# A hybrid decoder layer on one core: the order of wide and narrow products inside a projection block

## The chip, the core and the metric

The kernel runs on one core of a Trainium2 chip. A core has a matmul engine (TensorE, PE in the profile, with its weight loads shown as PEld), three elementwise engines (VectorE = DVE, ScalarE = ACT, GpSimd = POOL), queues of DMA transfers, an on-chip memory for operands, and a small accumulator memory (PSUM) that only matmuls accumulate in. The metric is the device time of one execution in microseconds. The median of three runs of the kernel before is 733.31 us (732.69 to 734.17).

A matmul here has a stationary operand of 128 x 128, loaded by an instruction of its own (LDWEIGHTS), and a moving operand of up to 512 columns. "Wide" below is a product with 512 moving columns, "narrow" one with 256.

## The reference

One decoder layer on 256 tokens of width 1024, in float32: a SwiGLU feed-forward, then a mixer with two branches side by side (Mamba-2 in chunks, and differential attention), merged by gates, then a second SwiGLU feed-forward; normalizations stand around each.

```python
def swiglu(x, w_gate, w_up, w_down):
    return (jax.nn.silu(x @ w_gate) * (x @ w_up)) @ w_down
...
    h = h + 0.5 * rmsnorm(swiglu(rmsnorm(h, ffn1_pre_g[l]), ...), ffn1_post_g[l])
    u = rmsnorm(h, mix_pre_g[l])
    z, xbc, dt_raw, q, k, v, gate_logits = jnp.split(u @ w_in[l], IN_SPLITS, axis=-1)
...
    h = h + rmsnorm(merged @ w_out[l], mix_post_g[l])
    h = h + 0.5 * rmsnorm(swiglu(rmsnorm(h, ffn2_pre_g[l]), ...), ffn2_post_g[l])
```

`xbc` holds the Mamba branch's x, B and C. The hidden width of the feed-forwards is 2816.

## The kernel before

**Precision.** Every float32 operand of a large product is split in two parts in a shorter matmul format (fp32r): hi is the rounded value, lo the rest. A product is then hi x hi + hi x lo + lo x hi. Weights are split on the core as they arrive: a chunk of 1 MB lands in a `raw` buffer (L240, on SP's queue), ScalarE casts each half to `whi` (L258), VectorE subtracts to give `wlo` (L259). Both halves lie in a ring of 29 equal buffers (`k4`), and `take` (L305) keeps the splitting three chunks ahead of use.

**The blocks in question.** The function `mm_w` (L334) makes the transposed output of one weight chunk of 1024 rows and 256 columns, in two blocks of 128 columns (`m`). The contraction runs over eight tiles `j`; `whi` and `wlo` each come as two halves of four tiles. The activations lie as hi and lo side by side, so that one wide product with `whi` as the stationary operand makes hi x hi in the left half of the accumulator and hi x lo in the right half (L342). A narrow product with `wlo` as the stationary operand adds lo x hi to the left half (L344). A block is eight wide products, then eight narrow ones, and an eviction: ScalarE copies the right half (L346 or L349), VectorE adds the left half (L347 or L350). Accumulators come from a PSUM ring of three (`pj`).

**Who calls it.** `mm_w` is called for gate and up of both feed-forwards (9 chunks each of gate and up, tiles `pg_f` and `pup_f`), for B and C (4 chunks, `pbc`), for x (8 chunks, `pxs`) and for q and k (4 chunks each, `pq` and `pk`): 56 chunks, 112 blocks. The other large products run elsewhere: V, the merge gates, the branch and output projections through `mm_nat` (L361), z through `mm_t` (L329 to L332, narrow products only), the first columns of gate and up of the first feed-forward through `mm_both` (L377), and the down projections through `mm_quads` (L718) and `mm_n` (L640). All of these but z use wide products.

**Order.** In parts of the program the order on TensorE is that of the source (`own_order`); in the parts where `mm_w` is called a scheduler orders the instructions of each engine, by dependencies and by times that it assumes. Between the projections of the mixer, pieces of other work (the chunked scan, the norms) are handed in by `back.run` (L1454) with a share of time each, and their matmuls stand between or inside blocks. Within a queue each engine issues in order.

Of the kernel before, what the change touches and what calls it, by code (L numbers as in the profile page):

```python
# [30 lines left out]
KD = D // P  # L31
# [23 lines left out]
def tile_hybrid_layer(ctx: ExitStack, tc: tile.TileContext, x, ffn1_pre_g, ffn1_w_gate, ffn1_w_up,  # L55
# [25 lines left out]
    def pj(name):  # L81

        return ps.tile([P, 512], F32, tag="pj", name=name, bufs=3)
# [250 lines left out]
    def mm_w(dst, name, w, act, scale=None):  # L334


        (wh, wl), (ah, _, ahl) = w, act
        for m in range(2):
            acc = pj(f"{name}{m}")
            cs = slice(m * P, (m + 1) * P)  # L340
            for j in range(KD):
                nc.tensor.matmul(acc, wh(j)[:, cs], ahl(j), start=j == 0, stop=False)  # L342
            for j in range(KD):
                nc.tensor.matmul(acc[:, :T], wl(j)[:, cs], ah(j), start=False, stop=j == KD - 1)  # L344
            if scale is None:
                nc.scalar.copy(dst[:, m, :], acc[:, T:])  # L346
                nc.vector.tensor_tensor(dst[:, m, :], acc[:, :T], dst[:, m, :], ALU.add)  # L347
            else:
                nc.scalar.activation(dst[:, m, :], acc[:, T:], AF.Copy, scale=scale)  # L349
                nc.vector.scalar_tensor_tensor(dst[:, m, :], acc[:, :T], scale, dst[:, m, :], ALU.mult, ALU.add)  # L350
# [483 lines left out]
    def ffn(post_v, tag, ready, turned, then, products):  # L834
# [28 lines left out]
        for j in range(2, FF // T):  # L863
            if j % 2 == 0:
                gh = k4([P, 4, T], f"gh_{tag}{j}", F32R)
                gl = k4([P, 4, T], f"gl_{tag}{j}", F32R)
            o = (j % 2) * 2
            gu += [(gh[:, o + m, :], gl[:, o + m, :]) for m in range(2)]
            sg = k2([P, 2, T], f"sg_{tag}{j}")
            mm_w(sg, f"pg_{tag}{j}", take(), act_u)  # L870
            act(sg, sg, AF.Silu)
            su = k2([P, 2, T], f"su_{tag}{j}")
            mm_w(su, f"pup_{tag}{j}", take(), act_u)
            nc.vector.tensor_tensor(sg, su, sg, ALU.mult)  # L874
            split(gh[:, o:o + 2, :], gl[:, o:o + 2, :], sg)
            if j // 2 in QUADS[tag]:
                if j % 2:
                    sums[j // 2] = sums_of(j // 2, even, sg)
                else:
                    even = sg  # L880
# [306 lines left out]
    for i in range(4):  # L1187
        acc = k2([P, 2, T], f"bc{i}")
        mm_w(acc, f"pbc{i}", take(), act_u)
        dst = (bT, cT)[i // 2]  # L1190
        conv(acc, 16 + 2 * i, dst[:, (i % 2) * 2:(i % 2) * 2 + 2, :])
        if i == 1:
            cumulated()
# [442 lines left out]
```

## Time and profile before

| | |
|---|---|
| median of three runs | 733.31 us |
| the profiled execution | 732.92 us |
| its span, first to last instruction | 731.1 us |
| mean granted TensorE clock | 0.997 |
| TensorE busy | 723.8 us, 4025 matmuls |
| VectorE busy | 607.6 us |
| ScalarE busy | 473.4 us |
| DMA | 137.92 MB, mean 189 GB/s |

Rows that group instructions give line, engine, operation, output and inputs by the program's names, shape, count, then busy time in us, the mean duration of one in ns, and the idle time before them. Rows in order of time give the start in us from the span's start, the length, and the same names; neighbours of one kind are merged with their count. Matmuls are pipelined: a product's duration is longer than the distance from its start to the next start, which is called its spacing below, and a busy TensorE is not one at its peak.

### The profile page before, as it was taken

The numbers are of one execution on the slowest core, as the hardware profiler recorded it, in microseconds if no ns is written. First come the engines' busy times: TensorE is split into PE (matmuls) and PEld (weight loads), VectorE is DVE, ScalarE is ACT, GpSimd is POOL, SyncE is SP. The second block draws the span as 40 slices with busy tenths as digits, with TensorE's granted clock in tenths as the row PEclk, the third lists the DMA queues.
The fourth block names the chain that finished last, engine by engine and source line by source line (L and its number), as shares of the span: only waits on it lengthen the run. The fifth ranks groups of instructions, "written<-read, shape, count | busy, mean of one in ns | idle before, by whom it ended". The sixth has DMA issues, their size and how long they took to land.

```text
span 731.1 us, 10546 instructions
## 1 busy us (share of the span) xinstructions
PE 723.8 (99%) x4025; PEld 620.9 (85%) x4025; DVE 607.6 (83%) x931; ACT 473.4 (65%) x805; POOL 31.3 (4%) x63
## 2 busy tenths in 40 slices
PE   9999999999999999999999999999999999999996
PEld 8888888888878889999888788888888888888885
DVE  6978788999979989777996997784784878779995
ACT  5657566656867676869965577782663757566562
POOL 4300000000200000000000000000010000000000
PEclk9999999999999999999999999999999999999998
DMA  8874645466673557675564664364461754654551
GB/s 296 235 261 147 225 158 188 173 225 264 184 227 119 172 173 226 206 226 180 158 221 148 203 220 144 144 243 190 126 240 37 231 193 155 228 203 146 181 189 57
DMA packets 94451, 137.92 MB, mean 189 GB/s; under 512 B 2669, under 2 KB 68801, under 8 KB 94401
## 3 DMA queue, kind: packets, MB, share of 16 engines
q1 hardware_dynamic: 91728, 129.51, 53.3%
q0 software_dynamic: 2368, 7.22, 3.3%
q8 instruction: 31, 0.51, 0.3%
q10 hardware_dynamic: 304, 0.53, 0.2%
q14 instruction: 20, 0.16, 0.1%
HBM read 136.17 MB, written 1.08 MB: 188 GB/s over the span
## 4 chain that ended last, share of the span: by engine, by line
PE 99%; DVE 0%; ACT 0%; DVEq 0%; issue 0%; ACTq 0%
PE pg_f L342 9%; PE pup_f L342 9%; PE pws L361 6%; PE pgt L361 6%; PE acc_f2p L718 5%; PE acc_f1p L718 5%; PE pup_f L344 5%; PE pg_f L344 5%; PE pxs L342 4%; PE pn_f L377 3%; PE acc_mx L640 3%; PE pn_mx L361 3%; PE pn_f L361 3%; PE pwd L361 3%; PE acc_f1p L640 2%; PE acc_f2p L640 2%
## 5 line engine op out<-in xcount | busy, mean ns | idle before, releaser
L259 DVE TENSOR_TENSOR wlo<-raw,whi 128x1024 fp32r<-128x1024 f32 x216 | 258.0, 1221 | 20.0 <-ACT whi L258 18.9
L258 ACT CAST whi<-raw 128x1024 fp32r<-128x1024 f32 x216 | 219.2, 1049 | 13.6 <-DMA raw<-in_ffn_w_down_dram 2.8
L342 PE MATMUL pg_f<-u_f,whi 128*128 128x512 f32 x288 | 72.9, 393 | 0.0
L342 PE MATMUL pup_f<-u_f,whi 128*128 128x512 f32 x288 | 72.1, 392 | 0.0
L342 PEld LDWEIGHTS pup_f<-u_f,whi 128*128 128x128 f32 x288 | 51.9, 189 | 9.5 <-issue 0.2
L342 PEld LDWEIGHTS pg_f<-u_f,whi 128*128 128x128 f32 x288 | 51.8, 189 | 9.2
L344 PEld LDWEIGHTS pg_f<-u_f,wlo 128*128 128x128 f32 x288 | 39.3, 190 | 2.8
L344 PEld LDWEIGHTS pup_f<-u_f,wlo 128*128 128x128 f32 x288 | 39.3, 190 | 2.8
L344 PE MATMUL pup_f<-u_f,wlo 128*128 128x256 f32 x288 | 40.2, 282 | 0.0
L344 PE MATMUL pg_f<-u_f,wlo 128*128 128x256 f32 x288 | 40.1, 282 | 0.0
L130 ACT CAST wqh<-wt 128x1024 fp32r<-128x1024 f32 x24 | 25.3, 1054 | 22.9 <-DVE wt L122 22.8
L346 ACT COPY su_f<-pup_f 128x256 f32<-128x256 f32 x36 | 13.4, 371 | 36.9 <-PE pup_f L344 36.9
L347 DVE TENSOR_TENSOR su_f<-pup_f,su_f 128x256 f32<-128x256 f32 x36 | 15.2, 421 | 24.9 <-ACT su_f L346 24.9
L361 PE MATMUL pgt<-whi,u_mx 128*128 128x512 f32 x128 | 33.1, 393 | 0.0
L342 PE MATMUL pxs<-u_mx,whi 128*128 128x512 f32 x128 | 32.4, 395 | 0.0
L329 PE MATMUL pz<-u_mx,whi 128*128 128x256 f32 x128 | 31.6, 284 | 0.0
L330 PE MATMUL pz<-u_mx,whi 128*128 128x256 f32 x128 | 31.5, 283 | 0.0
L135 DVE TENSOR_TENSOR wql<-wt,wqh 128x1024 fp32r<-128x1024 f32 x24 | 29.3, 1221 | 0.2
L361 PEld LDWEIGHTS pgt<-whi,u_mx 128*128 128x128 f32 x128 | 23.6, 188 | 5.3 <-issue 0.7
L342 PEld LDWEIGHTS pxs<-u_mx,whi 128*128 128x128 f32 x128 | 23.0, 189 | 4.1
L319 ACT CAST gh_f<-sg_f 128x512 fp32r<-128x512 f32 x18 | 11.2, 621 | 23.3 <-DVE sg_f L874 23.3
L135 DVE TENSOR_TENSOR wql<-raw,wqh 128x1024 fp32r<-128x1024 f32 x18 | 21.8, 1221 | 4.4 <-ACT wqh L130 4.4
(413 smaller groups left out, 1593.3 us busy)
## 6 DMA issues: line engine op xcount, KB each, us to landing
raw<-in_w_in_dram SPq DMA_DIRECT2D x40, 1024.0 KB, 5.2
raw<-in_ffn_w_down_dram SPq DMA_DIRECT2D x22, 1024.0 KB, 4.8
raw<-in_ffn_w_gate_dram SPq DMA_DIRECT2D x20, 1024.0 KB, 5.4
raw<-in_ffn_w_up_dram SPq DMA_DIRECT2D x20, 1024.0 KB, 5.1
raw<-in_ssd_w_branch_dram SPq DMA_DIRECT2D x8, 1024.0 KB, 4.9
acb<-acd POOLq DMA_DIRECT2D x8, 512.0 KB, 5.1
raw<-in_da_w_branch_dram SPq DMA_DIRECT2D x4, 1024.0 KB, 5.1
raw<-in_w_out_dram SPq DMA_DIRECT2D x4, 1024.0 KB, 4.8
```

Source lines behind the costliest of these rows:

```text
L130: nc.scalar.copy(hi, src)
L135: nc.vector.tensor_sub(lo, src, hi.bitcast(F32))
L258: last_cast[0] = behind(nc.scalar.copy(hi, r[:, js, :]), "cast").ins
L259: m = nc.vector.tensor_sub(lo, r[:, js, :], hi.bitcast(F32))
L329: nc.tensor.matmul(acc[m], wh(j)[:, cs], ah(k0 + j), start=first and j == ks[0], stop=False)
L330: nc.tensor.matmul(acc[m], wh(j)[:, cs], al(k0 + j), start=False, stop=False)
L342: nc.tensor.matmul(acc, wh(j)[:, cs], ahl(j), start=j == 0, stop=False)
L344: nc.tensor.matmul(acc[:, :T], wl(j)[:, cs], ah(j), start=False, stop=j == KD - 1)
L361: nc.tensor.matmul(acc, a(k0 + j), b(j), start=first and i == 0, stop=last and i == 11)
L377: nc.tensor.matmul(accs[b], x_(k0 + j), w_(j), start=first and j == 0 and w_ is wh and x_ is acts[b][0], stop=last and j == 3 and w_ is wl)
L640: nc.tensor.matmul(acc[b][q][:, cs] if to is None else to, x_[:, ts], w_(kt)[:, halves[q]][:, cs], start=to is not None and kt == 0 and x_ ...
L718: nc.tensor.matmul(bank[p], x_, w_, start=p not in begun, stop=last and p in (1, 5, 6, 7))
```

## The change

One line is removed, and with it one loop:

```diff
             for j in range(KD):
                 nc.tensor.matmul(acc, wh(j)[:, cs], ahl(j), start=j == 0, stop=False)
-            for j in range(KD):
                 nc.tensor.matmul(acc[:, :T], wl(j)[:, cs], ah(j), start=False, stop=j == KD - 1)
```

The wide product with `whi` and the narrow one with `wlo` of the same `j` now follow each other directly. A block reads wide, narrow, wide, narrow, eight times, and the last narrow product of a block is followed by the first wide one of the next. The number of products, their operands and their shapes stay the same; only the order of the additions into the left half changes. In the changed file all lines behind L342 have a number one lower, so the narrow products are at L343.

## The prediction

> **What bounds the kernel now.** I read the page first, then the waits of TensorE, then the groups by line, and last the order of time inside single blocks.
>
> ```profile
> span 731.1 us, 10546 instructions
> PE 723.8 (99%) x4025; PEld 620.9 (85%) x4025; DVE 607.6 (83%) x931; ACT 473.4 (65%) x805; POOL 31.3 (4%) x63
> PE 99%; DVE 0%; ACT 0%; DVEq 0%; issue 0%; ACTq 0%
> PE warm L451 <- DVE zeros L434: 1.1, 1, 1.1
> ```
>
> The first two rows are the span and the busy times. The third is the chain that ended last: TensorE is 99% of it. The fourth is the whole answer to "for whom did TensorE wait": one wait of 1.1 us at the very start. So the time is the sum of the spacings of the matmuls, and a change of their order can act only in two ways: through the spacing of neighbours, or by making TensorE wait for something that it now finds ready.
>
> The products that the change moves are these six groups at L342, each with as many at L344:
>
> ```profile
> L342 PE MATMUL pg_f<-u_f,whi 128*128 128x512 f32 x288 | 72.9, 393 | 0.0
> L342 PE MATMUL pup_f<-u_f,whi 128*128 128x512 f32 x288 | 72.1, 392 | 0.0
> L342 PE MATMUL pxs<-u_mx,whi 128*128 128x512 f32 x128 | 32.4, 395 | 0.0
> L342 PE MATMUL pbc<-u_mx,whi 128*128 128x512 f32 x64 | 16.4, 397 | 0.0
> L342 PE MATMUL pk<-u_mx,whi 128*128 128x512 f32 x64 | 16.4, 395 | 0.0
> L342 PE MATMUL pq<-u_mx,whi 128*128 128x512 f32 x64 | 16.3, 394 | 0.0
> L344 PE MATMUL pup_f<-u_f,wlo 128*128 128x256 f32 x288 | 40.2, 282 | 0.0
> ```
>
> 288 + 288 + 128 + 3 x 64 = 896 pairs of a wide (512) and a narrow (256) product, in 112 blocks of 8 pairs. One nanosecond on a pair is 0.9 us.
>
> **What a pair costs today.** From the order of time, a block's start and the start of the block 32 blocks later (in the first feed-forward, nothing between them but such blocks):
>
> ```profile
> 37.08 2.00 PE L342 MATMUL pup_f<-u_f,whi 128*128 128x512 f32 x8
> 38.92 1.11 PE L344 MATMUL pup_f<-u_f,wlo 128*128 128x256 f32 x8
> 39.87 0.40 PE L342 MATMUL pup_f<-u_f,whi 128*128 128x512 f32 x1
> ...
> 126.47 2.00 PE L342 MATMUL pup_f<-u_f,whi 128*128 128x512 f32 x8
> ```
>
> (126.47 - 37.08) / 32 = 2.793 us for a block, 349.2 ns for a pair: 1.84 us / 8 = 230 for a wide one, 0.95 us / 8 = 119 for a narrow one.
>
> **What each width costs when nothing changes around it.** A stretch of wide products only (24 starts from 24.78 to 30.22), and a stretch of narrow ones only (24 starts from 286.05 to 288.93):
>
> ```profile
> 24.78 1.98 PE L377 MATMUL pn_f<-whi,raw_u 128*128 128x512 f32 x8
> 30.22 0.62 PE L342 MATMUL pg_f<-u_f,whi 128*128 128x512 f32 x2
> L377 PE MATMUL pn_f<-whi,raw_u 128*128 128x512 f32 x15 | 3.9, 389 | 0.0
> ...
> 286.05 0.28 PE L329 MATMUL pz<-u_mx,whi 128*128 128x256 f32 x1
> 288.93 0.28 PE L329 MATMUL pz<-u_mx,whi 128*128 128x256 f32 x1
> L332 PE MATMUL pz<-u_mx,wlo 128*128 128x256 f32 x8 | 1.1, 283 | 0.0
> ```
>
> 5.44 us / 24 = 226.7 ns a wide one, shown with a duration of 389; 2.88 / 24 = 120.0 a narrow one, shown with 283. Duration less spacing is 162 or 163 in both, so a single product's spacing can be read off its duration. Together the steady prices make 346.7, 2.5 less than today's pair. The block at 62.22 shows where the 2.5 are (its first five wide products, one window each):
>
> ```profile
> L342 PE MATMUL pup_f<-u_f,whi 128*128 128x512 f32 x1 | 0.4, 396 | 0.0
> L342 PE MATMUL pup_f<-u_f,whi 128*128 128x512 f32 x1 | 0.4, 398 | 0.0
> L342 PE MATMUL pup_f<-u_f,whi 128*128 128x512 f32 x1 | 0.4, 389 | 0.0
> L342 PE MATMUL pup_f<-u_f,whi 128*128 128x512 f32 x1 | 0.4, 395 | 0.0
> L342 PE MATMUL pup_f<-u_f,whi 128*128 128x512 f32 x1 | 0.4, 393 | 0.0
> ```
>
> After a run of narrow products the wide ones cost 234, 236, 227, 233, 231 and then the settled 227. A disturbance outlives its cause by several products. The first narrow one after a settled wide one is cheap:
>
> ```profile
> L344 PE MATMUL pup_f<-u_f,wlo 128*128 128x256 f32 x1 | 0.3, 278 | 0.0
> ```
>
> 278 - 163 = 115, and the rest of its run is back at 120. So there is a settled price (wide 227, narrow 114) and a disturbed one (wide 231 to 236, narrow 120), some 6.5 ns apart for either width; a wide product needs about five of its kind to settle, one narrow product unsettles.
>
> **The change, step by step.** It removes and adds no instruction. Inside a block the order wide x8, narrow x8 becomes wide, narrow, eight times.
>
> *Spacing.* A wide product now always follows a narrow one, so it never gets the five it needs. I price it as disturbed for good. The row for that is the sum-products of the first feed-forward's down projection, where wide products alone are disturbed for 24 in a row:
>
> ```profile
> 134.82 0.63 PE L718 MATMUL acc_f1p<-wqh,s 128*128 128x512 f32 x2
> ...
> 140.42 0.39 PE L718 MATMUL acc_f1p<-wqh,gh_f 128*128 128x512 f32 x1
> ```
>
> (140.42 - 134.82) / 24 = 233.3 each. The narrow one follows a wide product that isn't settled. Two places show such a first narrow product: behind a single wide one at 368.4, and behind three at 32.5, in this order:
>
> ```profile
> L344 PE MATMUL pk<-u_mx,wlo 128*128 128x256 f32 x1 | 0.3, 281 | 0.0
> L344 PE MATMUL pg_f<-u_f,wlo 128*128 128x256 f32 x1 | 0.3, 285 | 0.0
> ```
>
> 281 - 163 = 118 and 285 - 163 = 122: not the cheap 115 that follows a settled one. I take their mean, 120, which is also the steady narrow price. The pair is then 233.3 + 120 = 353.3, against 349.2: +4.1 ns, times 896 = **+3.7 us**. No row of before alternates the widths, so the bounds: from below both settled, 226.7 + 114 = 340.7, -8.5 x 896 = -7.6 us; from above the dearest of each shown here, 236 + 122 = 358, +8.8 x 896 = +7.9 us. I take 353.3 because in every row here a product that follows a narrow or an unsettled one is disturbed.
>
> *Waits.* The first narrow product of a chunk now comes one wide product after the chunk's start (0.23 us), not eight (1.84), so half 0 of wlo is needed 1.6 us sooner; half 1 is needed after four pairs, 1.4 us, not 2.3. The split runs well ahead. The chunk whose block starts at 59.42 gets its wlo here:
>
> ```profile
> 48.73 1.22 DVE L259 TENSOR_TENSOR wlo<-raw,whi 128x1024 fp32r<-128x1024 f32 x1
> 50.20 1.22 DVE L259 TENSOR_TENSOR wlo<-raw,whi 128x1024 fp32r<-128x1024 f32 x1
> ```
>
> written by 51.42, 8 us ahead, so 1.6 us costs nothing. It would cost its full size if VectorE, 83% busy, had no such lead. The tightest place is the start of the second feed-forward:
>
> ```profile
> 566.50 1.23 DVE L259 TENSOR_TENSOR wlo<-raw,whi 128x1024 fp32r<-128x1024 f32 x1 [0.25 <-ACT whi L258]
> 567.49 1.30 PE L342 MATMUL pg_f<-u_f,whi 128*128 128x512 f32 x5
> 568.29 2.35 DVE L259 TENSOR_TENSOR wlo<-raw,whi 128x1024 fp32r<-128x1024 f32 x2
> ```
>
> Half 0 is there at 567.73 and half 1 at 568.29 + 2.35 / 2 = 569.47. In the changed order two wide products come first there, so the first narrow one is due at 567.95; half 1 is due after six wide, four narrow and four transposes (about 1.4 + 0.5 + 0.45), at 569.8. Both hold, by 0.2 and 0.3 us. I set 0, with a bound of 0.3 us. Were wlo late, everything behind it on TensorE's queue would stand still, for its products issue in order.
>
> *Buffers and evictions.* Half 0 of whi is last read at the middle of the chunk's second block as now, some 0.5 us later; half 0 of wlo about 1 us earlier. The weights that want these buffers are 8 us ahead, so neither is felt. The accumulator's last product is still the narrow one of j = 7, so the copy at L346 waits as it does. The transfers on SP's and GpSimd's queues keep their order: the changed program has the same rows there. VectorE's and ScalarE's differ in a few swaps of a conv step with a weight split, in the x stage; an eviction may come one split later (1.2 us), against a PSUM ring of three whose slot is due two blocks (5.6 us) on. Nothing.
>
> **Sum.** The profiled execution took 732.92 (span 731.1 and 1.8 around it): 732.92 + 3.7 = 736.6. It lies 0.4 below the median of the runs, 733.31; for the median I say **737.0 us**, +0.5%.
>
> **Rivals.** A difference of 0.2% (1.5 us) is about what a measurement of this kernel can tell from none.
>
> 1. *The steady prices simply add* (faster). The extra on the second to fifth wide product is paid only because wide ones follow each other after a narrow run; with one wide at a time, the 234 of the first and the cheap 114 of the next narrow one cancel: 346.7, -2.5 x 896 = -2.2 us, 731.1. For it: each long stretch holds one exact price, 226.7 or 120.0, and 234 + 114 is within 1.5 of their sum. It decides if a narrow product behind a single wide one gets the discount. Against: at 368.4 and 32.5 it didn't.
> 2. *Both settle* (faster): one narrow product is too little to disturb anything; 340.7 a pair, 725.7. Against: in the block the second narrow product already costs 120.
> 3. *Half way* (no change): the narrow price at the lower of the two rows, 118, and the wide one at the fourth to fifth of a run, 232: 350, +0.8 x 896 = +0.7 us, 734.0.
> 4. *Order plays no part* (no change): a product costs by its own columns alone, and the same products in another order take 349.2: 733.3. The durations from 389 to 398 for one shape speak against it.
> 5. *Dearer still* (slower): the dearest of each in turn, 358 a pair, 741.2. For it: 398 stands second in every run, just behind a product that followed a narrow one, which is where the narrow one will be.
>
> The Trainium skill, "TensorE: Matmul & The Clock Gate", section "Back-to-back issue gap", speaks for rival 4: columns / 2.4 + 2.5 ns, which would be an estimated 216 + 109 = 325 a pair in any order. The trace has 349.2 and neighbours that matter, so I give it little.
>
> **Chances.** The forecast 0.42, dearer still 0.09, steady prices 0.24, both settled 0.09, half way 0.12, order without part 0.04. Slower 0.51, same 0.16 (rivals 3 and 4), faster 0.33. The forecast's own range, 352 to 355.5 a pair with the 0.3 us of waiting, is 735.8 to 739.3. The range for 8 in 10 leaves out rival 2 and most of 5 and takes in rival 1: 730.6 to 739.5.
>
> **What would show it.** In the changed profile the duration of the 512-wide group tells the wide price (396 by the forecast; 389 if settled), that of the 256-wide group the narrow one (283; 278 if discounted), and the starts of two blocks 32 apart the pair (2.83 us a block; 2.77 by rival 1). TensorE's waits should stay at 1.1 us. If they grow at 567 or anywhere in the gate and up blocks, the step on wlo is wrong; if a block takes under 2.79, the step on spacing is.

## The result and the profile after

The changed kernel takes 735.67 us (median of six runs, 735.07 to 736.40), the kernel before in runs beside it 733.02 (six, 732.69 to 734.17). The ratio is 1.0041, with a 95% interval from 1.0031 to 1.0051: slower by 0.4%, 2.65 us by the medians. The profiled execution took 736.02.

The page and the waits of TensorE, after:

```profile
span 734.3 us, 10558 instructions
PE 725.9 (99%) x4025; PEld 619.2 (84%) x4025; DVE 608.0 (83%) x931; ACT 473.1 (64%) x805; POOL 30.8 (4%) x63
PE warm L450 <- DVE zeros L433: 1.1, 1, 1.1
PE pn_f L376 <- DVE whi L276: 0.7, 1, 0.7
PE pu_f L918 <- DMA h<-in_x_dram: 0.4, 1, 0.4
```

The span grew by 3.2 us and TensorE is as busy as it was. Two small waits are new, but both belong to the first transfers of the program, in front of all products that the change moves (the repeat of an unchanged kernel, further down, shows such waits coming and going from one execution to the next). Nothing waits in a gate, up, B, C, x, q or k block.

The same stretches of both kernels, each from its first product to the first of what follows: gate and up of the first feed-forward, B and C, x, q and k, gate and up of the second. (The last block of up stands behind two sum products of the down projection, L718 or L717, and so outside the first and the last stretch.) First before, then after. The columns are the stretch, its length, TensorE's busy time with its number of matmuls, its granted clock, the share of the DMA engines and GB/s.

```profile
30.22:129.26 99.04, 99.04 (x571) 1.00 0.59 198
214.62:238.72 24.10, 24.10 (x145) 1.00 0.49 151
238.72:286.05 47.33, 47.33 (x274) 1.00 0.57 179
340.56:392.49 51.93, 51.93 (x335) 1.00 0.66 213
567.49:665.67 98.18, 98.18 (x565) 1.00 0.58 194
```

```profile
30.61:130.87 100.26, 100.26 (x570) 1.00 0.59 196
216.06:240.01 23.95, 23.95 (x144) 1.00 0.50 155
240.01:287.74 47.73, 47.73 (x274) 1.00 0.58 183
342.25:394.42 52.17, 52.17 (x334) 1.00 0.66 212
569.46:668.87 99.41, 99.41 (x565) 1.00 0.57 191
```

The clock is 1.00 everywhere, so this is spacing and not throttling. The two gate and up stretches grew by 1.22 and 1.23 us: 280 pairs in each, so 4.4 ns a pair, near the 4.1 of the forecast. But B and C became *shorter* by 0.15, and x and q and k grew by 0.40 and 0.24 where 128 pairs at 4.1 would give 0.52 each. The groups of the moved products show the same:

```profile
L342 PE MATMUL pg_f<-u_f,whi 128*128 128x512 f32 x288 | 102.7, 399 | 0.0
L342 PE MATMUL pxs<-u_mx,whi 128*128 128x512 f32 x128 | 45.7, 400 | 0.0
L342 PE MATMUL pbc<-u_mx,whi 128*128 128x512 f32 x64 | 22.5, 394 | 0.0
L343 PE MATMUL pup_f<-u_f,wlo 128*128 128x256 f32 x288 | 80.9, 281 | 0.0
```

A wide product lasts 399 in gate and 394 in B and C, for the same shape and the same neighbours. (Busy time per group is larger than before only because two products that overlap are now of two groups.) The order of time gives both prices exactly. Fifteen chunks of the first feed-forward, 240 pairs, and fifteen pairs of the first x chunk, in the kernel after:

```profile
43.25 0.40 PE L342 MATMUL pg_f<-u_f,whi 128*128 128x512 f32 x1
128.05 0.40 PE L342 MATMUL pup_f<-u_f,whi 128*128 128x512 f32 x1
...
240.01 0.39 PE L342 MATMUL pxs<-u_mx,whi 128*128 128x512 f32 x1
245.21 0.39 PE L342 MATMUL pxs<-u_mx,whi 128*128 128x512 f32 x1
```

(128.05 - 43.25) / 240 = 353.33 ns a pair; (245.21 - 240.01) / 15 = 346.7. So strict alternation has two prices, and a stretch that no other product interrupts keeps one of them once it has begun. The dear one is a cycle of three pairs. Two windows of 20 ns in the kernel after, at 60.20 and at 65.85, each over the border of two blocks so that the names keep neighbours apart:

```profile
L342 PE MATMUL pg_f<-u_f,whi 128*128 128x512 f32 x1 | 0.4, 403 | 0.0
L342 PE MATMUL pup_f<-u_f,whi 128*128 128x512 f32 x1 | 0.4, 398 | 0.0
L343 PE MATMUL pg_f<-u_f,wlo 128*128 128x256 f32 x1 | 0.3, 284 | 0.0
...
L342 PE MATMUL pup_f<-u_f,whi 128*128 128x512 f32 x1 | 0.4, 398 | 0.0
L342 PE MATMUL pg_f<-u_f,whi 128*128 128x512 f32 x1 | 0.4, 395 | 0.0
L343 PE MATMUL pup_f<-u_f,wlo 128*128 128x256 f32 x1 | 0.3, 277 | 0.0
```

With the 162 that a wide duration has over its spacing: 241, 236, 233, and again. Their mean is 236.7, and the narrow ones between them make 116.7. In the cheap pattern no wide product costs over 233. Counted over the trace, 756 of the 896 pairs ran in the dear pattern (gate and up without their last blocks, 112 of x, 84 of q and k) and 140 in the cheap one (all of B and C, the first x chunk, five and a half blocks of q and k, and the last block of each gate and up stage). The five stretches hold the 756 and 124 of the others: 756 x 4.1 - 124 x 2.5 = +2.8 us, against 323.52 - 320.58 = 2.94 by their sums. By exclusion, the other 0.1 is in the irregular pairs where a stretch starts and around transposes.

### The profile page after: what moved, and what is told of

Same layout as the page of the kernel before. It is cut to its first block, busy times and chain, and to the rows that moved or that the text cites. A ratio compares the mean times of both kernels' runs of the same rounds, so it can differ in the third digit from the quotient of the medians.

```text
span 734.3 us, 10558 instructions
## 1 busy us (share of the span) xinstructions
PE 725.9 (99%) x4025; PEld 619.2 (84%) x4025; DVE 608.0 (83%) x931; ACT 473.1 (64%) x805; POOL 30.8 (4%) x63
## 4 chain that ended last, share of the span: by engine, by line
PE 98%; DMA 1%; DVE 0%; SPq 0%; ACT 0%; DVEq 0%; issue 0%; ACTq 0%
PE pg_f L342 9%; PE pup_f L342 9%; PE pgt L360 6%; PE pws L360 6%; PE acc_f1p L717 5%; PE acc_f2p L717 5%; PE pg_f L343 5%; PE pup_f L343 5%; PE pxs L342 4%; PE acc_mx L639 3%; PE pn_mx L360 3%; PE pn_f L360 3%; PE pwd L360 3%; PE pn_f L376 3%; PE acc_f1p L639 2%; PE acc_f2p L639 2%
## 5 line engine op out<-in xcount | busy, mean ns | idle before, releaser
L342 PE MATMUL pg_f<-u_f,whi 128*128 128x512 f32 x288 | 102.7, 399 | 0.0
L342 PE MATMUL pup_f<-u_f,whi 128*128 128x512 f32 x288 | 102.6, 398 | 0.0
L343 PE MATMUL pup_f<-u_f,wlo 128*128 128x256 f32 x288 | 80.9, 281 | 0.0
L343 PE MATMUL pg_f<-u_f,wlo 128*128 128x256 f32 x288 | 80.8, 281 | 0.0
L342 PEld LDWEIGHTS pup_f<-u_f,whi 128*128 128x128 f32 x288 | 54.1, 188 | 13.5 <-issue 0.2
L342 PEld LDWEIGHTS pg_f<-u_f,whi 128*128 128x128 f32 x288 | 54.1, 188 | 13.3
L343 PEld LDWEIGHTS pg_f<-u_f,wlo 128*128 128x128 f32 x288 | 54.4, 189 | 0.2
L343 PEld LDWEIGHTS pup_f<-u_f,wlo 128*128 128x128 f32 x288 | 54.4, 189 | 0.1
L342 PE MATMUL pxs<-u_mx,whi 128*128 128x512 f32 x128 | 45.7, 400 | 0.0
L343 PE MATMUL pxs<-u_mx,wlo 128*128 128x256 f32 x128 | 35.9, 281 | 0.0
L342 PEld LDWEIGHTS pxs<-u_mx,whi 128*128 128x128 f32 x128 | 24.1, 188 | 5.7
```

## The experiments

Most versions write the order of a block as a string (w a wide product, n a narrow one) and leave all else of the changed kernel as it is:

```diff
-            for j in range(KD):
-                nc.tensor.matmul(acc, wh(j)[:, cs], ahl(j), start=j == 0, stop=False)
-                nc.tensor.matmul(acc[:, :T], wl(j)[:, cs], ah(j), start=False, stop=j == KD - 1)
...
+            at = {"w": 0, "n": 0}
...
+            for k in ORDERS[calls[0]][m]:
+                j = at.get(k)
+                if k == "w":
+                    mm = nc.tensor.matmul(acc, wh(j)[:, cs], ahl(j), start=j == 0, stop=False)
+                elif k == "n":
+                    mm = nc.tensor.matmul(acc[:, :T], wl(j)[:, cs], ah(j), start=False, stop=j == KD - 1)
...
```

Each time below stands beside that of the kernel before on the same chip. It is a single run where no number of runs is given, and a median otherwise; the last column has the lengths of the first and the last of the five stretches.

| run | what differs | us | before | gate/up, 1st and 2nd |
|---|---|---|---|---|
| run lengths | several orders in the first feed-forward | 733.60 | 732.71 | 99.35, 98.20 |
| disturbances | single swaps; extra small products | 738.24 | 732.71 | 99.43, 105.86 |
| pad | the kernel before, rings 64 bytes higher | 732.46 | 732.71 | 99.03, 98.20 |
| eight swaps | swaps meant to lock the cheap pattern | 731.98 (11 runs) | 732.63 | 98.47, 97.69 |
| two and two | wwnn throughout | 732.76 | 732.63 | 98.81, 98.05 |
| sixteen | both blocks of a chunk open | 733.98 | 732.63 | 99.42, 98.61 |
| rings low | the kernel before, rings in another place | 732.75 | 732.63 | 99.03, 98.19 |
| reset, 3rd pair | settled blocks, then a swap | 734.27 (10 runs) | 732.69 | 100.22, 99.29 |
| eight swaps again | a second trace | 731.66 | 732.69 | 98.46, 97.67 |
| alternation, rings low | the changed kernel, rings in another place | 734.19 | 732.69 | 100.27, 97.59 |
| reset, 2nd pair | settled blocks, then a swap one pair sooner | 730.76 (7 runs) | 732.70 | 98.48, 97.57 |
| the same, rings low | and the rings in another place | 731.91 (10 runs) | 732.70 | 98.49, 97.56 |

### Run lengths

```diff
+ORDERS = (
+    [('wwnnwwnnwwnnwwnn', 'wwnnwwnnwwnnwwnn')] * 6 +
+    [('wwwwnnnnwwwwnnnn', 'wwwwnnnnwwwwnnnn')] * 6 +
+    [('wwnwnwnwnwnwnwnn', 'wwnwnwnwnwnwnwnn')] * 6 +
+    [('wnwnwnwnwnwnwnwn', 'wnwnwnwnwnwnwnwn')] * 20 +
+    [('wwwwwwwwnnnnnnnn', 'wwwwwwwwnnnnnnnn')] * 18)
```

> The changed kernel with other run lengths, one for each stretch of chunks: in the first feed-forward's gate and up six chunks of wide x2, narrow x2, then six of wide x4, narrow x4, then six of two wide first and then narrow and wide in turn; B, C, x, q, k alternate as in the changed kernel; the second feed-forward has wide x8, narrow x8. Theory (a disturbance is started by one narrow product and needs about five wide ones to end): a pair costs 352 to 353.5 ns in runs of two, 350.5 to 351.5 in runs of four, 353.3 in the last six chunks, 349.2 in the second feed-forward. Rival (a loss of a fixed 20 ns for every change from narrow to wide, as the block of before has 2793 ns against 8 x 346.7): 356.7 in runs of two, 351.7 in runs of four. Rival (steady prices add, and only the stretch's beginning decides between 346.7 and 353.3): some of the three orders settle at 346.7. Span of the whole by the theory 0.2 to 1.0 us below the changed kernel's 734.3.

The starts at which one order gave way to the next, in its trace (five chunks of two and two, six of four and four, five of the third order):

```profile
37.38 0.40 PE L354 MATMUL pup_f<-u_f,whi 128*128 128x512 f32 x1
65.25 0.40 PE L354 MATMUL pg_f<-u_f,whi 128*128 128x512 f32 x1
98.91 0.40 PE L354 MATMUL pg_f<-u_f,whi 128*128 128x512 f32 x1
127.08 0.40 PE L354 MATMUL pup_f<-u_f,whi 128*128 128x512 f32 x1
```

Two and two: 27.87 / 80 = 348.4. Four and four: 33.66 / 96 = 350.6. One narrow behind, with two wide at a block's head and two narrow at its end: 28.17 / 80 = 352.1. Beside them eight and eight at 349.2 and alternation at 353.3 or 346.7. If a change of width had a price of its own, these would rise with the number of changes (2, 4, 8, 14, 16 a block: 349.2, 350.6, 348.4, 352.1, 353.3 or 346.7). They don't. The price belongs to the whole repeating sequence. The theory of five wide products to settle missed at two and two (352 to 353.5 expected) and in the third order (353.3), the fixed price per change missed at two and two (356.7) and four and four (351.7), and none of the three orders went to 346.7.

### Disturbances

In the first feed-forward every other chunk begins with one swap, wwnn, in place of wnwn (later wwwnnn); in the second, 1, 2 or 4 products of zeros, 128 wide, stand ahead of the block.

```diff
+    [('wnwnwnwnwnwnwnwn', 'wnwnwnwnwnwnwnwn')] * 1 +
+    [('wwnnwnwnwnwnwnwn', 'wnwnwnwnwnwnwnwn')] * 1 +
...
+    [('dwnwnwnwnwnwnwnwn', 'wnwnwnwnwnwnwnwn')] * 1 +
...
+            kick = bg([P, P], f"kick{name}{m}") if "d" in ORDERS[calls[0]][m] else None
...
+                    mm = nc.tensor.matmul(kick, zeros, zeros, start=True, stop=True)
```

> The changed kernel's trace holds two steady patterns for the same alternation: wide 233, 241, 236 with narrow 117, 120, 113 (353.3 a pair, both feed-forwards) and wide 230 with narrow 117 (346.7 a pair, B, C, the first chunks of x and part of q and k). Here chunks of gate and up get a disturbance at their start, every second chunk: in the first feed-forward two wide and two narrow first (three times), then three and three (four times); in the second one, two or four extra 128-wide float32 products of zeros into an unused accumulator. Theory (two patterns, which one is kept is set by how the stretch begins and it then lasts until the next interruption): some of the disturbances switch the stretch behind them to 346.7, and it stays there over the undisturbed chunk that follows; a feed-forward that spends half its pairs there gains 288 / 2 x 6.7 ns = 1.0 us less the extra products at 0.11 us each. Rival (the cheap pattern belongs to the mixer's stages, by their neighbours on other engines or their memory): every chunk here stays at 353.3 whatever the start; the span is that of the changed kernel, 734.3, plus the extra products (some 28 x 0.11 = 3 us).

The third swap of this trace (at 59.64) and the starts of a chunk before and behind it; the row at 70.73 is where the next swap begins:

```profile
53.99 0.40 PE L383 MATMUL pg_f<-u_f,whi 128*128 128x512 f32 x1
...
59.64 0.63 PE L383 MATMUL pup_f<-u_f,whi 128*128 128x512 f32 x2
...
65.19 0.40 PE L383 MATMUL pg_f<-u_f,whi 128*128 128x512 f32 x1
...
70.73 0.63 PE L383 MATMUL pup_f<-u_f,whi 128*128 128x512 f32 x2
```

5.65 / 16 = 353.1 ahead of the swap, 5.54 / 16 = 346.3 a chunk later. The instructions, tiles and operands are of the same kind on both sides, and one exchange of neighbours moved everything behind it to the other price. The next swap, at 70.73, moved it back. Of the eight swaps the first, third, fifth and seventh began in the dear pattern and ended in the cheap one, the others the reverse. So there are two patterns, the same chunks of gate and up run in either, and a stretch keeps what its start led into; the rival, by which the cheap pattern belongs to the mixer's stages, is refuted. The products of zeros led to the dear pattern four times and to the cheap one five times, and nine cases show no rule. They make the second gate and up stretch 7.7 us longer; 2.8 of that is the last block of up, which in this kernel stands ahead of the first sum product and so inside the stretch.

### Pad and rings low

The prediction took its wide price from the sum products of L718. Two runs ask what makes those dear. Both use the kernel before. One shifts the rings of 2 KB and 3 KB tiles by 64 bytes:

```diff
+    pad = []
...
+        if not pad:
+            pad.append(sb.tile([P, 16], F32, tag="pad", name="pad", bufs=1))
+            nc.gpsimd.memset(pad[0], 0.0)
```

> The kernel before with an unused buffer of 64 bytes a partition in front of the two small rings in which the sum-products' stationary operands lie, so that these start at a multiple of 128 bytes instead of 64 beyond one; nothing else moves. It asks what the 233.3 ns of the wide sum-products in the down projection is due to, from which the forecast took its price. Theory A (the place of the stationary operand within 128 bytes): all wide products there fall to 226.7, 24 of them in each of two groups of a down projection and some ten behind them; a down projection gets 0.4 to 0.5 us shorter, the whole 0.8 to 1.0. Theory B (what the operands are, or the ring as such): the 233.3 stay and the span is 731.1 within 0.3.

With the pad, the wide products on the sums sh last 389, 392 and 404 (minimum, median and maximum of 18), against 389, 393 and 398 before. They are not settled, but the pattern is another: 231 and 236 in turn became a longer cycle with single products of 241. Their mean over the same 24 starts is still 232.9. So moving the rings to a multiple of 128 bytes, which by the expectation might have settled them, doesn't, but the place has some say. The other run lays these rings ahead of the 4 KB ring:

```diff
+    for early in (k3, k2):
+        nc.gpsimd.memset(early([P, 16], "early"), 0.0)
```

> The kernel before with the rings of 2 KB and 3 KB tiles laid out ahead of the 4 KB ring, so that the sums and their products' stationary tiles start at 36864 and above instead of 215872 and above in a partition; order and instructions otherwise unchanged but for two small memsets. Theory place (products of the same width cost 233 where their operands lie in that ring and 226.7 where not): the 48 sum products of the first two groups of each down projection, 231 and 236 in turn before, settle at 226.7, 96 x 6.6 = -0.6 us, 732.1. Rival (it is the sums' order, three accumulators in turn and operands shared, whatever their place): 231 and 236 stay, 732.7 within 0.2.

The stretch that the prediction priced at (140.42 - 134.82) / 24 = 233.3, and the first waits of TensorE:

```profile
134.72 0.62 PE L721 MATMUL acc_f1p<-wqh,s 128*128 128x512 f32 x2
...
140.16 0.39 PE L721 MATMUL acc_f1p<-wqh,gh_f 128*128 128x512 f32 x1
...
PE acc_f1p L643 <- DVE wlo L262: 0.3, 1, 0.3
```

(140.16 - 134.72) / 24 = 226.7: settled, with the same instructions in the same order. The other traces bear it out: these 24 starts average 232.9 to 233.3 in both down projections of all eleven traces with the rings behind the 4 KB ring, and 226.7 in both of all three traces with the rings ahead of it. The dear L718 row was a matter of where its operands lie, not of their order. The time didn't show it (732.75, where 732.1 was expected): 0.3 us of the gain in the first feed-forward went into a wait on a late split, and the rest is below what one run can tell.

### Eight swaps, twice

Swaps at eight places, one early in each feed-forward, four in x, two in q and k:

```diff
+    [('wnwnwnwnwnwnwnwn', 'wnwwnnwnwnwnwnwn')] * 1 +
...
+    [('wnwnwwnnwnwnwnwn', 'wnwnwnwnwnwnwnwn')] * 4 +
...
+    [('wwnnwnwnwnwnwnwn', 'wnwnwnwnwnwnwnwn')] * 1 +
```

> The changed kernel with eight places where one pair of neighbours is swapped (wide narrow wide narrow becomes wide wide narrow narrow): once early in each feed-forward's gate/up, once in each of the four x chunks that follow an interruption, twice in q and k. Theory two patterns (alternation has a dear pattern of 353.3 ns a pair and a cheap one of 346.7, and one swap in the dear one throws it into the cheap one, which then lasts until the next interruption): both gate/up stages leave the dear pattern after the first chunk, some 275 pairs x 6.7 = 1.8 us each, x 0.5 to 0.7, q and k 0.2 to 0.4; the time is 730.6 to 731.6, 0.2 to 0.3% under the kernel before, and the profile shows wide starts of 230 to 233 behind the swap. Rival from the prediction (the price goes by what precedes a product, three neighbours and no more): eight swaps move eight pairs by a few ns, and the time stays at 735.6.

731.98 against 732.63, a ratio of 0.9997 (0.9988 to 1.0006): 0.4 above the expected range, and by its interval no gain over the kernel before. The mechanism held and the locks in x did not all hold: gate and up fell to 98.47 and 97.69 from 100.26 and 99.41, but in x two of the four swaps began at a wide product of 230 or 231, as the cheap pattern has them, and the dear pattern followed, so x took 47.52, not 47.0. The executions spread from 731.42 to 733.48, which one trace can't explain; so a second one:

> The eight swaps of the earlier run once more, for a second trace of the same instructions. Theory two patterns with starts set by the instructions alone: the same pattern in every stretch as in the first trace, gate/up at 98.5 and 97.7 us, time 731.4 to 732.0. Rival (the start of a stretch depends on when data arrives, so the pattern differs from one execution to the next, which would be the spread of 731.42 to 733.48): one or both gate/up stages at 100.2 and 99.4, time 732.8 to 733.5.

```profile
30.30:128.76 98.46, 98.46 (x570) 1.00 0.60 200
566.83:664.50 97.67, 97.67 (x565) 1.00 0.59 195
...
PE pu_f L944 <- DMA h<-in_x_dram: 0.7, 1, 0.7
```

The stages repeat within 0.02 us, with the same pattern behind each of the eight swaps. So a start is set by the instructions ahead of it, in these two executions. Three kernels that have the same unswapped alternation in B, C and x (the changed one, run lengths and disturbances) agree as well: 23.95 and 47.73 us in each, within 0.01. The row on h is a wait at the program's start that the first trace of the same kernel hasn't got: its first gate product came 24.9 us behind the first one of the norm, there 24.0. Up to 0.9 us of the spread can come from there; the rest of the 2 us stays open.

### Two and two, and sixteen

Two other orders that don't depend on a pattern's start:

```diff
+    [('wwnnwwnnwwnnwwnn', 'wwnnwwnnwwnnwwnn')] * 56)
```

> Two wide and two narrow products in turn in all seven matrices. Theory two patterns (the price belongs to the whole repeating sequence; two and two was read at 348.4 a pair in the first six chunks of an earlier run): 896 x (348.4 - 349.2) = -0.7, so 732.0 on a chip where the kernel before takes 732.7. Rival (each change of width costs, so half as many changes as in alternation lie half way between 353.3 and eight and eight at 349.2): 351.2 a pair, 734.5.

```profile
65.17 0.40 PE L350 MATMUL pg_f<-u_f,whi 128*128 128x512 f32 x1
...
120.90 0.40 PE L350 MATMUL pg_f<-u_f,whi 128*128 128x512 f32 x1
```

(120.90 - 65.17) / 160 = 348.3, as read before, and the five stretches together are 0.6 us shorter than before. The whole was not: 732.76 in one run, 0.8 over the expectation, with 0.2 more at the program's start and 0.35 behind the last gate and up stage, where a product waits for an eviction. The other one opens both blocks of a chunk:

```diff
+        accs = [pj(f"{name}{m}") for m in range(2)]
         for m in range(2):
-            acc = pj(f"{name}{m}")
+            acc = accs[m]
...
+        for m in range(2):
+            acc = accs[m]
+            cs = slice(m * P, (m + 1) * P)
             for j in range(KD):
                 nc.tensor.matmul(acc[:, :T], wl(j)[:, cs], ah(j), start=False, stop=j == KD - 1)
```

> Both blocks of a chunk open at once: sixteen wide products, then sixteen narrow, with two accumulators held. Half as many changes of width as the kernel before has. If the settling behind a change is the whole loss of eight and eight (40 ns a block over 8 x 346.7 = 2773.6, by 2793 read), a chunk loses 20 less: 56 x 0.02 = -1.1 us, so 731.6 where the kernel before takes 732.7; the evictions of a chunk's two blocks come together and cost nothing. Rival: the two blocks' late evictions hold up the third accumulator, waits of 0.3 us or more in front of a chunk's second block, and the time is 733 or more.

Two undisturbed chunks, and the waits of the weight loads:

```profile
110.10 0.40 PE L343 MATMUL pg_f<-u_f,whi 128*128 128x512 f32 x1
...
121.24 0.40 PE L343 MATMUL pg_f<-u_f,whi 128*128 128x512 f32 x1
...
PEld pup_f L343 <- DVE sg_f L351: 1.9, 7, 0.3
```

11.14 / 32 = 348.1 where nothing waits: the spacing gained what was expected. But the rival held for the whole. Three accumulators are too few for two that stay open: seven times the next block's first weights waited for VectorE's addition of L351, an eviction (1.9 us in all on the loads, some 0.2 each on the products), and the time was 733.98.

### Reset, then a swap

Narrow products that have settled (the z stage) were followed by the dear pattern in all traces that alternate there. So eight and eight in one block makes the start known, and a swap behind it should lead out. First at the third pair:

```diff
+    [('wnwnwnwnwnwnwnwn', 'wwwwwwwwnnnnnnnn')] * 1 +
+    [('wnwnwwnnwnwnwnwn', 'wnwnwnwnwnwnwnwn')] * 1 +
...
+    [('wwwwwwwwnnnnnnnn', 'wwwwwwwwnnnnnnnn')] * 1 +
+    [('wnwnwwnnwnwnwnwn', 'wnwnwnwnwnwnwnwn')] * 1 +
```

> The changed kernel with the swaps placed behind a reset: the first chunk of each feed-forward keeps eight wide and eight narrow in its second block (in the second feed-forward in both), so that alternation begins on settled narrow products, which was followed by the dear pattern in all four traces (z to q), and the swap stands at the third pair behind it; in x one swap alone, in the chunk behind the first interruption; in q and k one at the start of q and one at the start of the last k chunk. Theory two patterns: gate/up 98.5 and 97.8 us by stage, x 47.0, q and k 51.6, together 1.0 us less than the kernel before in B to k and 0.9 in the two gate/up stages; 730.9 to 731.5 where the kernel before takes 732.6, and executions spread less than 1.2 us. Rival (the pattern behind a swap is drawn anew in each execution): median within 0.5 us of the kernel before, spread of 2 us as with the swaps alone (731.42 to 733.48).

734.27 us, 1.0021 (1.0012 to 1.0031): 2.8 over the expected range, all of it in gate and up. In x and in q and k the same run met its numbers (47.02 and 51.67). The order of time at the swap in the first feed-forward, and fifteen chunks behind it:

```profile
36.65 0.40 PE L360 MATMUL pup_f<-u_f,whi 128*128 128x512 f32 x1
37.00 0.40 PE L360 MATMUL pup_f<-u_f,whi 128*128 128x512 f32 x1
37.36 0.62 PE L360 MATMUL pup_f<-u_f,whi 128*128 128x512 f32 x2
...
42.29 0.40 PE L360 MATMUL pg_f<-u_f,whi 128*128 128x512 f32 x1
127.09 0.40 PE L360 MATMUL pup_f<-u_f,whi 128*128 128x512 f32 x1
```

84.80 / 240 = 353.33: the swap did nothing. The difference to swaps that worked is where in the cycle of three it stands. Behind the reset the wide products run 233, 241, 236, and the third pair is the one of 236. All swaps that had ended the dear pattern before began at a 241 or a 233. The same version with the swap one pair sooner, in both feed-forwards:

```diff
-    [('wnwnwwnnwnwnwnwn', 'wnwnwnwnwnwnwnwn')] * 1 +
+    [('wnwwnnwnwnwnwnwn', 'wnwnwnwnwnwnwnwn')] * 1 +
```

> As the version with the reset, but in both feed-forwards the swap stands one pair earlier. The dear pattern runs 233, 241, 236 in turn; every swap so far that began at a 241 or at a 233 threw it into the cheap pattern, and both that began at a 236 (third pair behind the reset) left it dear. Theory phase (the swap works by the place in the cycle of three at which it stands): behind the reset the second pair is the 241, so gate/up falls from 100.2 and 99.3 us to 98.5 and 97.8, and the time lies 3.2 under that version, 730.6 to 731.4 where the kernel before takes 732.7. Rival (the settled block ahead of it is what keeps the dear pattern, wherever the swap stands): gate/up stays at 100.2 and 99.3 and the time at 734.2.

```profile
37.52 0.40 PE L360 MATMUL pup_f<-u_f,whi 128*128 128x512 f32 x1
37.87 0.64 PE L360 MATMUL pup_f<-u_f,whi 128*128 128x512 f32 x2
...
43.09 0.39 PE L360 MATMUL pg_f<-u_f,whi 128*128 128x512 f32 x1
126.29 0.39 PE L360 MATMUL pup_f<-u_f,whi 128*128 128x512 f32 x1
```

83.20 / 240 = 346.67, over the same fifteen chunks. One pair of difference in where two neighbours are exchanged is worth 3.5 us to the kernel (1.58 over the kernel before in the one set of runs, 1.94 under it in the other). 730.76 us (730.05 to 731.49) is 0.9973 of the kernel before, 0.9962 to 0.9985: this version beats both kernels, the one before by 0.3%. Over all traces, 24 swaps wwnn in the dear pattern began at a 241 or a 233, and all 24 ended it; the two that began at a 236 did not. Many of the 24 are one place in several versions, some have only one or two pairs ahead of them, and a 236 was tried at the third pair behind a reset alone; a swap at a 236 far from a reset is not tested.

### Alternation and swaps with the rings moved

Both add the edit that lays the rings low, the first to the changed kernel, the second to the last version.

> The changed kernel, no swaps, with the rings of 2 KB and 3 KB tiles laid out ahead of the 4 KB ring, as in the earlier run of the kernel before that let its sum products settle at 226.7. Theory two patterns set by how a stretch begins, whatever the operands' place: gate/up stays at 353.3 a pair in both feed-forwards, about 735.5. Rival (the dear pattern, like the 233 of the sum products, comes from where the operands lie): gate/up falls to 346.7 a pair, 98.3 and 97.5 us, and the time to 732.0 or less.

Gate and up of both feed-forwards in the first of them:

```profile
30.90:131.17 100.27, 100.27 (x571) 1.00 0.59 197
569.38:666.97 97.59, 97.59 (x566) 1.00 0.59 195
```

Neither side is met whole. The first feed-forward kept the dear pattern with its operands in another place, so the place doesn't make it. The second went into the cheap pattern without any swap, and the kernel took 734.19. Its wide and narrow products come in the same order there as in the changed kernel, but the first narrow one already takes 120, not 116. So the price isn't fixed by the place, yet where the buffers lie can change how a stretch starts; one run shows it, and by what way is open. With the reset and the swap together with the moved rings:

> The same, with the rings of 2 KB and 3 KB tiles laid out ahead of the 4 KB ring. Theory place for the sums and phase for the swaps act each by itself: gate/up as in the run beside it, and the 96 sum products of both down projections at 226.7 instead of 233.3, 0.6 us less, 730.0 to 730.8, unless a late weight takes 0.3 of it back as it did in the kernel before with these rings. Rival (moving the rings moves the start of the stretches too, so that the swap falls on another place of the cycle): one gate/up stage at 100 and the time 1 us or more over the run beside it.

Gate and up took 98.49 and 97.56, so reset and swap act at both places, and the sum products cost 226.7 in both down projections. The time of 730.0 to 730.8 that was expected did not come. The median of 731.91, 0.9992 (0.9983 to 1.0001) is yet 1.1 over the run beside it, while its profiled execution had the shortest span of all, 729.3. In q and k the pattern began dear again (52.01 against 51.67), which is 0.3 of it; what took the rest in the other executions isn't known.

## Why the prediction came out right, point by point

- **What bounds the kernel: right.** TensorE's spacing is the time. All of the loss is in the spacing of the moved products, 2.94 us in five stretches.
- **Waits, buffers, evictions at nothing: right.** The profile shows no wait at L342 or L343, at 569 neither. The earlier reading of wlo had its lead.
- **The pair at 353.3: right in sum, in gate and up.** Blocks there take 8 x 353.33 = 2.83 us, the number given. The two parts were off in opposite ways: wide 236.7, not 233.3 (the group shows 399, not 396), narrow 116.7, not 120 (281, not 283).
- **The row behind the wide price: the wrong one.** "I price it as disturbed for good" rested on the sum products of L718. These are dear because of where their operands lie; with the rings moved they cost 226.7. That the dear pattern comes to the same sum within 0.1 ns was luck.
- **"A product that follows a narrow or an unsettled one is disturbed": fell.** That is the step that failed. In the cheap pattern each wide product follows a narrow one and the pair costs as much as the two settled prices added, 346.7 (at 240, wide 230 and narrow 116.7, neither of them the settled price). The prediction's own rows spoke against it: at 62.22 the third wide product lasts 389, as the settled ones do, right behind one of 398. The first rival's price was real, but its condition (the discount of the narrow product behind a single wide one) was not what decides; the start of the stretch does.
- **All 896 pairs at one price: wrong.** 140 ran at 346.7, 6.6 ns less: 0.9 us of the 1.3 by which 737.0 was too much. Another 0.3 is the median that it was counted from (733.31 of three runs, 733.02 of six). The measured 735.67 lies 0.1 under the 735.8 at which the forecast's own range began.
- **Order plays no part (fourth rival): refuted.** The same products cost 346.7, 348.4, 349.2, 350.6, 352.1 or 353.3 a pair. The columns / 2.4 + 2.5 of the Trainium skill, "TensorE: Matmul & The Clock Gate", section "Back-to-back issue gap", which that section gives for an isolated matmul, would be an estimated 325 a pair. No order here comes down to that; the measured prices decide.
- **Both settle, half way, dearer still (second, third and fifth rivals): not seen.** No stretch of alternation kept 340.7, 350 or 358 a pair. Single wide products do reach 241, above the dearest row of before, but the cycle's mean is 353.3.

The prediction held both prices, one as the forecast and one as a rival of the other sign. Which of them a stretch takes can't be read from the profile of before, where nothing alternates. So the sign came out as forecast partly by luck: with a few settled blocks and swaps at the right places, nearly the same alternation takes 730.76.

## What to carry to other kernels

In this kernel, where TensorE is busy 99% of the time, the order of products of different widths moved the time by some tenths of a per cent, and the price was that of the whole repeating sequence. Read such a price from two starts many repetitions apart, not from a rule on neighbours. The alternation had two steady prices, and how a stretch began decided which one it kept. Where that may be so, make the start a known one (a settled run ahead of it), try one exchange of neighbours at each place of the cycle, and read from the trace which exchange changed the price. A row that is borrowed for a price should come from the same cause: one run with the buffers moved would have shown that the borrowed one did not.

## What the runs showed of the hardware

- Strict alternation of 512 and 256 columns has two steady prices here, 353.33 and 346.67 ns a pair, and keeps one for 240 pairs and more. Settled wide products cost 226.7, narrow ones 120.0.
- The steady prices are whole multiples of 6.67 ns: 53, 52, 34 and 18 of them in the order just given, and a block of eight and eight at 2793 ns is 419. The two patterns of alternation differ by one such step in each pair. That something in the issue of matmuls moves in steps of this size is an inference from the numbers; no run here isolates it.
- The spacing of equal wide products depends on where their operands lie: 233.3 with the small rings laid out behind the 4 KB ring, 226.7 with them ahead of it, the order being the same. Which property of the place it is stays open; a shift of 64 bytes changed the pattern and left the mean at 232.9.
